# Idle products and new order edges at the start of a hybrid decoder step

## The chip, the cores and the metric

One Trainium2 chip, and on it one core. The metric is the device time of one execution in microseconds (us); a time is the median of several runs. The engines are PE (TensorE, matrix products), ACT (ScalarE), DVE (VectorE), POOL (GpSimd) and SP (SyncE, which only issues transfers). ACT and POOL issue transfers too; a queue that waits to issue one holds up the compute instructions behind it.

## What is computed

One layer of a hybrid decoder for 512 prompt tokens and 8 x 8 sample tokens (576 columns in all), all in float32:

```
h = x + 0.5 * SwiGLU_1(rms(x))                      # first FFN, 1024 -> 2816 -> 1024
u = rms(h) @ W_in -> z | xBC | dt | q | k | v | f | g_ssd | g_att
y_ssd = Mamba-2 SSD(z, xBC, dt)                     # causal conv of 4 on x/B/C, chunked scan, gate, group norm
y_att = FoX attention(q, k, v, f)                   # samples attend 2048 cached positions in pages
h = h + W_out(sigmoid(g_ssd) * (y_ssd @ W_ssd_proj) + sigmoid(g_att) * (y_att @ W_attn_proj))
y = h + 0.5 * SwiGLU_2(rms(h))                      # second FFN
```

The outputs are y for both groups, the new keys, values and log forget rows, and the new SSD and convolution states.

## The kernel before

The hidden state lies transposed in SBUF, features on the 128 partitions, the 576 tokens in the columns, in 8 tiles `hts[k]`. Every large product is made in three passes of one-pass float32 (`mm3`): each operand is split into a rounded half and the rest (`whi`, `wlo` for weights, `xh`, `xl` for activations), and the three products hi x hi, hi x lo and lo x hi are added (lines L208, L209, L210). Each pass takes 128 x 128 weights against 288 columns, half of the tokens. Weights come by SP's queue as `stage` tiles of 512 KB; ACT makes `whi` (L173), DVE or POOL `wlo` (L174).

The order of the stages: x is loaded in two column halves on the queues of SP and ACT, with the first gate weights between them. PE transposes it (L432 for prompt rows, L438 for sample rows), the copies go to `hts` (L434 on ACT, L436 and L439 on DVE), and `Norm.add` makes `xh` (L220, ACT) and `xl` (L221, DVE). ACT squares the rows of x (L446) for the norm; a short chain on DVE and four small products give the scale `nrm1.r`, by which the accumulators of the first FFN are multiplied as they leave PSUM. Then come setup loads of small weights (`bb` L488 and L489, `al` L493, and rows), the state_conv rows `sc` with 24 small transposes (L515) and their store, and the cached log forget rows: a gather `lg` (L524), 16 scans `pf` on DVE (L529), one product with the page matrix (L535), 16 subtractions on POOL (L540) and 32 stores `pastD` on ACT's queue (L546).

The FFN (`ffn`) goes over 22 tiles f of 128 hidden features: gate product, silu, up product, and the product of both split again into `hh` and `hl`; after 12 and after the last 10 tiles the down projection over 8 output tiles j. Accumulators come from `acc()`, which in the FFN alternates between two `acc` banks and two `pv` banks; two `tr` banks and two `mm` banks (`sm()`) serve transposes and small products. After each f and each j the FFN advances a generator `beside` by one step: here `turns(4)`, which loads tiles of the SSD state (`h0`, called h in the trace), transposes them (L376) and stores them.

Attention runs in 37 hand-ordered steps on PE; each handles a quarter of a sample's cached keys (`turn_keys`: transposes L924, copies `kT` on ACT L926; scores L935) and one query block of a prompt pair (`scores`: products L861, exps on ACT L867; turns L879; values L892), with products of the gates and of z filled in between. Behind attention the sample columns of its results are copied from `ys` on POOL (L1114). Then six convolution tiles of the first SSD group follow (`conv_tile`: POOL copy L1129, accumulators to `xr` on DVE L1133 to L1140, a transpose L1146 and its copy L1148 on ACT), and the attention projection with the split results `yh` (L217) and `yl` (L218).

The order of the instructions on each engine is made by a planner: it simulates the program with costs of its own and takes, among what is ready, what stands first in the code; `soon()` raises a priority. In attention PE's order is that of the code.

Of the kernel before, what the change touches and what calls it, by code (L numbers as in the profile page):

```python
# [16 lines left out]
I32 = mybir.dt.int32  # L17
# [76 lines left out]
def build(ctx, tc, A, O):  # L94
# [58 lines left out]

    def hs(half):
        return slice(half * HT, (half + 1) * HT)
# [56 lines left out]
    def hilo(hp, view, tagh, tagl, scale=None, n=NT, bufs=None):  # L212

        hi = tl(hp, [P, n], F32R, tag=tagh, bufs=bufs)
        lo = tl(hp, [P, n], F32R, tag=tagl, bufs=bufs)
        if scale is None:
            act(hi, view, AF.Copy)  # L217
            V.tensor_tensor(lo, view, hi.bitcast(F32), ALU.subtract)  # L218
        else:
            act(hi, view, AF.Copy, scale=scale)  # L220
            V.scalar_tensor_tensor(lo, view, scale, hi.bitcast(F32), ALU.mult, ALU.subtract)  # L221
        return hi, lo
# [45 lines left out]
    class Norm:  # L268


        def __init__(self, wcol, sqp=None, xsp=xp):
            self.wcol, self.xs, self.n, self.sqp, self.xsp = wcol, [], 0, sqp, xsp

        def add(self, h, squares=True):
            k = self.n
            self.xs.append(hilo(self.xsp, h, "xh", "xl", scale=P1[:, self.wcol + k:self.wcol + k + 1]))
# [36 lines left out]
    def ffn(nrm, cg, wu, wd, hts, done, beside):  # L313

        cu = Cols(wu, 0)
        with pool("hid", reuse_waits="tile") as hidp, pool("ffnt", bufs=2, reuse_waits="tile") as fp:
            for lo_f, hi_f in ((0, 12), (12, NF)):
                hid = []
                for f in range(lo_f, hi_f):
# [5 lines left out]
                    for half in range(2):  # L325
                        a = acc()
# [38 lines left out]
    def turns(wait):  # L365
# [42 lines left out]

    with pool("h1", reuse_waits="tile") as hp:
        hts = [tl(hp, [P, NT], tag=f"h{k}") for k in range(8)]  # L410
        nrm1 = Norm(0)
        with pool("xin", side="right", reuse_waits="tile") as xi:
# [16 lines left out]
            for k in range(8):  # L429
                t = tr()  # L430
                for c in range(4):
                    nc.tensor.transpose(t[:, c * P:(c + 1) * P], xin[c][:, k * P:(k + 1) * P], ident)  # L432
# [10 lines left out]
            for c in range(5):  # L443
                n = P if c < 4 else NS
                junk = tl(xi, [P, D], tag="junk")
                act(junk[:n], xin[c][:n], AF.Square, accum_out=x0[:n, c:c + 1])  # L446
# [4 lines left out]
        with pool("setup2", side="right", reuse_waits="tile") as su:  # L451
# [36 lines left out]
            q.dma_start(out=bb[:32], in_=A["dt_bias"].rearrange("o h -> h o"))  # L488
            q.dma_start(out=bb[32:48], in_=A["b_f"].rearrange("o h -> h o"))  # L489
# [3 lines left out]
            q.dma_start(out=al[:32], in_=A["a_log"].rearrange("o h -> h o"))  # L493
# [14 lines left out]
            sc = tl(su, [24, CONV], tag="sc")  # L508
            for j in range(3):
                q.dma_start(out=sc[j * B:(j + 1) * B], in_=A["state_conv"][0, :, j, :])  # L510
            scT = tl(su, [P, 24, 24], tag="scT")
            for j in range(0, 24, 12):
                t = tr()
                for i in range(12):
                    nc.tensor.transpose(t[:, i * 24:(i + 1) * 24], sc[:, (j + i) * P:(j + i + 1) * P], ident[:24, :24])  # L515
                V.tensor_copy(scT[:, j:j + 12, :], t[:, :288].rearrange("p (i c) -> p i c", c=24))
            q.dma_start(out=scD, in_=scT)


        with pool("lg", side="right", reuse_waits="tile") as lp:  # L520
            pcol = tl(lp, [P, 1], I32, tag="pcol")
            nc.scalar.dma_start(out=pcol, in_=A["page_table"].rearrange("b n -> (b n)").unsqueeze(1))
            lg = tl(lp, [P, P, 16], tag="lg")
            G.indirect_dma_start(out=lg.rearrange("p s h -> p (s h)"), out_offset=None,  # L524
                                 in_=A["cache_logf"].rearrange("o n s h -> (o n) (s h)"),
                                 in_offset=bass.IndirectOffsetOnAxis(ap=pcol[:, :1], axis=0))
            pf = tl(lp, [P, 16, P], tag="pf")
            for h in range(16):
                V.tensor_tensor_scan(pf[:, h, :], C("one"), lg[:, :, h], 0.0, ALU.mult, ALU.add)  # L529
            tot = tl(lp, [P, 16], tag="tot")  # L530
            V.tensor_copy(tot, pf[:, :, P - 1])
            t = sm()
            page = tl(lp, [P, P], tag="page")
            nc.scalar.dma_start(out=page, in_=A["consts"][:, COFF["page"][0]:COFF["page"][0] + P])
            mm(t[:, :16], lhsT=page, rhs=tot, start=True, stop=True)  # L535
            st = tl(lp, [P, 16], tag="st")
            V.tensor_copy(st, t[:, :16])

            for h in range(16):
                G.tensor_tensor(lg.rearrange("p s h -> p (s h)")[:, h * P:(h + 1) * P].rearrange("p (q r u) -> p r q u", q=4, u=4),  # L540
                                pf[:, h, :].rearrange("p (r q u) -> p r q u", q=4, u=4),
                                st[:, h:h + 1].unsqueeze(2).unsqueeze(3).to_broadcast([P, 8, 4, 4]), ALU.subtract)
            lv = lg.rearrange("p s h -> p (s h)").rearrange("p (h q e) -> p h q e", h=16, q=4)
            for b in range(B):
                for q in range(4):
                    nc.scalar.dma_start(out=pastD[b, :, q].rearrange("h g e -> g h e"), in_=lv[b * NPG:(b + 1) * NPG, :, q, :])  # L546
# [955 lines left out]
```

## Time and profile before

| | |
|---|---|
| median of 3 runs | 1887.17 us (1885.02 to 1891.32) |
| the profiled execution | 1890.57 us, span 1888.4 us |
| PE busy | 1834.7 us (97%) |
| DVE, ACT, POOL busy | 1062.6, 746.2, 606.5 us |
| mean transfer rate | 143 GB/s |

A span is the time between the first and the last instruction of the profile; the execution is a little longer. Rows of the profile name line, engine, operation, tile written and tiles read. A row of a timeline begins with start and duration; in brackets at its end stand the idle time ahead of it and what ended that. A row of a window stands for a stretch: its length, then busy time and instructions of PE, PEld (weight loads of PE), DVE, ACT and POOL, the granted clock of PE, the share of the transfer engines and GB/s.

### The profile page before, as it was taken

What the parts mean: (1) busy time and instruction counts of PE and PEld (TensorE: products, weight loads), DVE (VectorE), ACT (ScalarE), POOL (GpSimd) and SP (SyncE); (2) the same over time, 40 slices, a digit from 0 to 9 for tenths busy, and PEclk for the clock granted to TensorE, in tenths of its full rate; (3) what the DMA queues carried; (4) which work ended last, traced back from release to release, by engine and by line L of the source; (5) the groups of instructions that cost most, each with busy time, mean ns of one, the idle gap of its engine ahead of it and who ended that gap; (6) DMA issues with size and microseconds to landing.
All of it is one profiled execution on the core that took longest, in us unless ns stands there. A gap on an engine that the chain in (4) does not pass through costs nothing.

```text
span 1888.4 us, 38769 instructions
## 1 busy us (share of the span) xinstructions
PE 1834.7 (97%) x15335; PEld 1729.5 (92%) x15335; DVE 1062.6 (56%) x2309; ACT 746.2 (40%) x1555; POOL 606.5 (32%) x681
## 2 busy tenths in 40 slices
PE   7999999999999999999999999999999999999998
PEld 7999999999889787888899898888989999999998
DVE  4544234434425677777655968787695544444442
ACT  4233223334323545545335645454433333223322
POOL 0432003322322344443323735656553332002210
PEclk9999999999999999999999999999999999999999
DMA  5453443445525678775456545354463444444432
GB/s 154 107 147 124 134 124 112 124 146 142 140 79 167 184 223 228 233 217 156 117 144 189 151 113 149 98 152 143 134 210 90 118 130 133 144 132 125 117 119 67
DMA packets 297722, 269.71 MB, mean 143 GB/s; under 512 B 55068, under 2 KB 262092, under 8 KB 297388
## 3 DMA queue, kind: packets, MB, share of 16 engines
q1 hardware_dynamic: 229712, 184.16, 34.9%
q10 hardware_dynamic: 57828, 46.10, 7.9%
q0 software_dynamic: 10000, 36.97, 6.3%
q8 instruction: 121, 1.98, 0.5%
q14 instruction: 61, 0.50, 0.1%
HBM read 223.72 MB, written 38.73 MB: 139 GB/s over the span
## 4 chain that ended last, share of the span: by engine, by line
PE 83%; DVE 7%; DMA 3%; ACT 3%; issue 2%; POOL 1%; ACTq 1%; SPq 0%; DVEq 0%; POOLq 0%
PE acc L208 16%; PE acc L209 16%; PE acc L210 15%; PE pv L209 8%; PE pv L208 8%; PE pv L210 7%; PE tr L935 2%; PE tr L924 1%; PE mm L861 1%; DMA ab<-cumD 1%; PE pv L892 1%; DVE kf L1159 1%; PE mm L879 1%; PE pv L973 1%; PE tr L376 1%
## 5 line engine op out<-in xcount | busy, mean ns | idle before, releaser
L173 ACT ACTIVATE whi<-stage 128x512 fp32r<-128x512 f32 (+2 forms) x474 | 294.7, 622 | 713.0 <-PE acc L209 605.2
L208 PE MATMUL acc<-xh,whi 128*128 128x288 f32 x1792 | 542.3, 303 | 8.4 <-ACT tt L1148 3.6
L209 PE MATMUL acc<-xl,whi 128*128 128x288 f32 x1792 | 533.8, 298 | 0.0
L210 PE MATMUL acc<-xh,wlo 128*128 128x288 f32 x1792 | 533.0, 298 | 0.0
L174 DVE TENSOR_TENSOR wlo<-stage,whi 128x512 fp32r<-128x512 f32 (+1 forms) x373 | 260.7, 699 | 268.1 <-ACT whi L173 251.1
L208 PEld LDWEIGHTS acc<-xh,whi 128*128 128x128 f32 x1792 | 339.5, 189 | 15.7 <-ACT tt L1148 7.7
L209 PEld LDWEIGHTS acc<-xl,whi 128*128 128x128 f32 x1792 | 339.7, 190 | 2.9 <-issue 2.7
L210 PEld LDWEIGHTS acc<-xh,wlo 128*128 128x128 f32 x1792 | 338.9, 189 | 1.1 <-issue 0.5
L174 POOL TENSOR_TENSOR wlo<-stage,whi 128x512 fp32r<-128x512 f32 (+1 forms) x101 | 138.4, 1370 | 287.7 <-ACT whi L173 275.5
L341 POOL TENSOR_TENSOR u<-u,s 128x288 f32<-128x288 f32 x88 | 81.5, 927 | 437.2 <-DVE u L340 379.8
L208 PE MATMUL pv<-xh,whi 128*128 128x288 f32 (+1 forms) x720 | 214.2, 298 | 1.7 <-ACT xh L220 1.5
L209 PE MATMUL pv<-xl,whi 128*128 128x288 f32 (+1 forms) x720 | 213.1, 296 | 0.0
L210 PE MATMUL pv<-xh,wlo 128*128 128x288 f32 (+1 forms) x720 | 212.6, 295 | 0.0
L208 PEld LDWEIGHTS pv<-xh,whi 128*128 128x128 f32 (+1 forms) x720 | 135.3, 188 | 2.3 <-ACT xh L220 1.8
L209 PEld LDWEIGHTS pv<-xl,whi 128*128 128x128 f32 (+1 forms) x720 | 135.1, 188 | 1.3
L210 PEld LDWEIGHTS pv<-xh,wlo 128*128 128x128 f32 (+1 forms) x720 | 135.2, 188 | 0.2
L208 PE MATMUL pv<-hh,whi 128*128 128x288 f32 x352 | 105.7, 300 | 0.0
L343 POOL TENSOR_TENSOR hl<-u,hh 128x288 fp32r<-128x288 f32 x88 | 79.4, 904 | 80.4 <-ACT hh L342 80.4
L209 PE MATMUL acc<-hl,whi 128*128 128x288 f32 x352 | 104.1, 296 | 0.0
L208 PE MATMUL acc<-hh,whi 128*128 128x288 f32 x352 | 104.1, 296 | 0.0
L209 PE MATMUL pv<-hl,whi 128*128 128x288 f32 x352 | 104.1, 296 | 0.0
L210 PE MATMUL acc<-hh,wlo 128*128 128x288 f32 x352 | 104.1, 296 | 0.0
(364 smaller groups left out, 3618.0 us busy)
## 6 DMA issues: line engine op xcount, KB each, us to landing
stage<-in_w_in_dram SPq DMA_DIRECT2D x52, 512.0 KB
stage<-in_ffn_w_up_dram SPq DMA_DIRECT2D x44, 512.0 KB
stage<-in_ffn_w_gate_dram SPq DMA_DIRECT2D x43, 512.0 KB
stage<-in_ffn_w_down_dram SPq DMA_DIRECT2D x40, 512.0 KB
h<-in_state_ssm_dram SPq DMA_DIRECT2D x64, 256.0 KB
hTD<-hT ACTq DMA_DIRECT2D x32, 256.0 KB
pb<-pastD SPq DMA_DIRECT2D x32, 256.0 KB
ab<-cumD SPq DMA_DIRECT2D x32, 256.0 KB
```

The lines of the kernel that those rows point to most:

```text
L173: act(hi, view, AF.Copy)
L174: e.tensor_tensor(lo, view, hi.bitcast(F32), ALU.subtract)
L208: mm(out, lhsT=hi, rhs=a, start=first and i == 0, stop=False)
L209: mm(out, lhsT=hi, rhs=b, start=False, stop=False)
L210: mm(out, lhsT=lo, rhs=a, start=False, stop=last and i == n - 1)
L341: G.tensor_tensor(u, u, sil[half], ALU.mult)
L343: G.tensor_tensor(hl[:, hs(half)], u, hh[:, hs(half)].bitcast(F32), ALU.subtract)
L376: nc.tensor.transpose(ps[:, b * P:(b + 1) * P], h0[:, b, :], ident)
L861: mm(s[:, :n], lhsT=q, rhs=ks[2 * self.p + e][:, :n], start=hl == 0, stop=hl == 1)
L879: nc.tensor.transpose(t[:, j * P:(j + 1) * P], lt[:, j * P:(j + 1) * P], ident)
L892: mm(self.ob[o:o + 32, i * P:(i + 1) * P], lhsT=vtok[j][:, v0:v0 + 32], rhs=self.pts[e][:, j * P:(j + 1) * P], start=j == 0, stop=j == i)
L935: mm(s[kv * 32:(kv + 1) * 32, :], lhsT=self.q(kv), rhs=self.kT[kv // 2], start=True, stop=True)
```

## The change

- Six products of a constant tile (448 columns, plain float32) are put on PE ahead of the transposes of x.
- A helper `behind(later, first)` adds an edge of order between two instructions. With it the first three squares of x stand behind the 4th, 6th and 7th `xh`, the loads of `bb` and `al` behind the 8th; the other two squares are made on DVE.
- The gate products of f=1 use a `tr` and an `mm` bank.
- The work on `sc` and `lg` moves into a generator `aside`, which the FFN advances beside its tiles; after it come the state turns, with `h0` loaded two tiles ahead.
- In each first quarter of attention the two exps stand behind the key copies.
- The sample copies of `ys` and the splits `yh`, `yl` stand behind the third convolution tile; `ys` lies in another pool.

```diff
+    def behind(later, first):
+        tc.add_manual_dep(later.ins, first.ins.name, mybir.DependencyInfo(mybir.DependencyClass.NoSync, mybir.DependencyReason.DATA), reason="order")
...
-                        a = acc()
+                        a = (tr, sm)[half]()[:, :HT] if f in more else acc()
...
+            tiles = []
             for t in range(16):
                 for h in range(2):
-                    h0 = tl(sp_, [P, 4, P], tag="h0", bufs=4)
-                    nc.sync.dma_start(out=h0, in_=ap3(A["state_ssm"][0], *place(h, t)))
+                    for n in range(len(tiles), min(2 * t + h + 3, 32)):
+                        tiles.append(tl(sp_, [P, 4, P], tag="h0", bufs=4))
+                        nc.sync.dma_start(out=tiles[n], in_=ap3(A["state_ssm"][0], *place(n % 2, n // 2)))
+                    if t + h == 0:
+                        yield
+                    h0 = tiles[2 * t + h]
...
+    idle = tl(tp, [P, NT], tag="sq", bufs=1)
+    V.memset(idle, 1.0)
+    warm = [mm(pv()[:, :NT - P], lhsT=idle[:, NT - P:], rhs=idle[:, :NT - P], start=True, stop=True) for _ in range(6)]
...
-                    nc.tensor.transpose(t[:, c * P:(c + 1) * P], xin[c][:, k * P:(k + 1) * P], ident)
+                    x = nc.tensor.transpose(t[:, c * P:(c + 1) * P], xin[c][:, k * P:(k + 1) * P], ident)
+                    if k == 0:
+                        behind(x, warm[-1])
...
-                act(junk[:n], xin[c][:n], AF.Square, accum_out=x0[:n, c:c + 1])
+                if c < 3:
+                    behind(act(junk[:n], xin[c][:n], AF.Square, accum_out=x0[:n, c:c + 1]), nrm1.insts[2 * c + 3 - c // 2])
+                else:
+                    V.tensor_tensor_reduce(junk[:n], xin[c][:n], xin[c][:n], 1.0, 0.0, ALU.mult, ALU.add, x0[:n, c:c + 1])
...
-            q.dma_start(out=bb[:32], in_=A["dt_bias"].rearrange("o h -> h o"))
+            behind(q.dma_start(out=bb[:32], in_=A["dt_bias"].rearrange("o h -> h o")), nrm1.insts[7])
...
+        def aside():
+            with pool("rows", side="right", reuse_waits="tile") as su:
+                sc = tl(su, [24, CONV], tag="sc")
+                for j in range(3):
+                    nc.scalar.dma_start(out=sc[j * B:(j + 1) * B], in_=A["state_conv"][0, :, j, :])
+                yield
+                yield
...
+            with pool("lg", side="right", reuse_waits="tile") as lp:
...
+                for _ in range(2):
+                    yield
...
+            yield from turns(1)
...
-        ffn(nrm1, cg, A["ffn1_w_up"][0], A["ffn1_w_down"][0], hts, done1, turns(4))
+        ffn(nrm1, cg, A["ffn1_w_up"][0], A["ffn1_w_down"][0], hts, done1, aside(), (1,))
...
-        ys = tl(ap, [P, 2, 4, NS], tag="ys")
+        ys = tl(yp, [P, 2, 4, NS], tag="ys")
...
-                        act(self.kT[p], t, AF.Copy)
+                        copy = act(self.kT[p], t, AF.Copy)
+                    for x in exps:
+                        behind(x, copy)
...
-                    new.turn_keys(jq)
+                    new.turn_keys(jq, cur.exps if jq == 0 else ())
...
-        for p in range(2):
-            for g in range(4):
-                G.tensor_copy(yt[p * 4 + g][:, NP:], ys[:, p, g, :])
...
+        convs.append((first, tanh, last))
...
-            yhl = [hilo(yhp, y, "yh", "yl", bufs=8) for y in yt]
+            yhl = []
+            for n, y in enumerate(yt):
+                c = G.tensor_copy(y[:, NP:], ys[:, n // 4, n % 4, :])
...
+                h = act(hi, y, AF.Copy)
+                for x, first in zip((c, h, V.tensor_tensor(lo, y, hi.bitcast(F32), ALU.subtract)), convs[2]):
+                    behind(x, first)
+                yhl.append((hi, lo))
```

More of the change, by code (lines that the diff above doesn't have):

```diff
@@ L219, in hilo @@
         else:
-            act(hi, view, AF.Copy, scale=scale)
+            h = act(hi, view, AF.Copy, scale=scale)
             V.scalar_tensor_tensor(lo, view, scale, hi.bitcast(F32), ALU.mult, ALU.subtract)
+            if insts is not None:
+                insts.append(h)
         return hi, lo
@@ L310, in build, with ffn @@
     upbD = tl(dram, [4, 2, NS, P], tag="upbD")
-    def ffn(nrm, cg, wu, wd, hts, done, beside):
+    def ffn(nrm, cg, wu, wd, hts, done, beside, more=()):
         cu = Cols(wu, 0)
@@ L492, in build @@
             V.memset(al, 0.0)
-            q.dma_start(out=al[:32], in_=A["a_log"].rearrange("o h -> h o"))
+            behind(q.dma_start(out=al[:32], in_=A["a_log"].rearrange("o h -> h o")), nrm1.insts[7])
             act(al, al, AF.Exp)
@@ L506, in build @@
             V.tensor_tensor(pidx, pf32.unsqueeze(2).to_broadcast([P, B, 4]), rq.unsqueeze(1).to_broadcast([P, B, 4]), ALU.add)
[L508 to L546, printed above, removed]
@@ L853, in scores @@
                 n = (i + 1) * P
-                self.lts = []
+                self.lts, self.exps = [], []
                 for e in range(2):
```

53 lines of the change are left out of this document (44 added, 9 removed).

## The prediction

> **What bounds the kernel now.** I read the page first. TensorE (PE) is busy for nearly the whole span, and the chain that ended last is 83% PE, so time can come only from PE's waits and from products that PE runs slowly.
>
> ```profile
> span 1888.4 us, 38769 instructions
> PE 1834.7 (97%) x15335; PEld 1729.5 (92%) x15335; DVE 1062.6 (56%) x2309; ACT 746.2 (40%) x1555; POOL 606.5 (32%) x681
> ```
>
> The span less PE's busy time is 53.7 us. The view of waits on PE says for whom (line, who released it, us in total, times, longest):
>
> ```profile
> PE tr L935 <- ACT kT L926: 5.2, 6, 1.1
> ...
> PE acc L208 <- ACT tt L1148: 3.8, 8, 1.8
> ...
> PE tr L257 <- POOL ssq L1246: 3.2, 1, 3.2
> ...
> PE tr L376 <- DMA h<-in_state_ssm_dram: 2.8, 1, 2.8
> ...
> PE tr L515 <- DMA sc<-in_state_conv_dram: 1.8, 1, 1.8
> ...
> PE mm L535 <- DVE tot L531: 1.3, 1, 1.3
> ...
> PE acc L1146 <- POOL xr L1129: 1.3, 1, 1.3
> ```
>
> All but L257 lie in places that the diff touches: the row work before the first FFN (L515, L535, L376), attention (L935), and the first convolution tiles after it (L1148, L1146). The fourth place is the start. A wait has a second price, which the stretches by window show (us, PE busy, ..., granted clock):
>
> ```profile
> 14.78:33.11 18.33, 18.33 (x115) 17.39 (x116) 13.07 (x34) 13.72 (x25) 0.00 (x0) 1.00 0.32 95
> 33.11:35.34 2.23, 1.66 (x13) 1.29 (x11) 1.80 (x4) 1.41 (x4) 0.00 (x0) 1.00 0.20 17
> 103.85:110.40 6.55, 3.71 (x18) 3.74 (x18) 2.44 (x4) 1.86 (x5) 4.27 (x5) 0.74 0.76 222
> 921.90:930.00 8.10, 5.39 (x27) 5.20 (x28) 6.85 (x12) 4.50 (x9) 1.56 (x3) 0.79 0.01 2
> ```
>
> Around the waits for L376 and for the convolution tiles the granted clock averages 0.74 and 0.79: a half-rate spell. The timeline of PE shows what half rate is in the start, where the clock column says 1.00 all the same:
>
> ```profile
> 17.04 0.44 PE L208 MATMUL pv<-xh,whi 128*128 128x288 f32 x1
> 17.28 0.44 PE L209 MATMUL acc<-xl,whi 128*128 128x288 f32 x1
> 24.20 0.29 PE L208 MATMUL pv<-xh,whi 128*128 128x288 f32 x1
> 24.33 0.30 PE L209 MATMUL pv<-xl,whi 128*128 128x288 f32 x1
> 52.42 0.44 PE L209 MATMUL pv<-xl,whi 128*128 128x288 f32 x1
> 55.30 0.44 PE L209 MATMUL pv<-xl,whi 128*128 128x288 f32 x1
> ```
>
> From start to start a product of 288 columns takes 0.24 us at half rate, 0.13 us else. From 52.42 to 55.30 thirteen products are slow: 13 x 0.11 = 1.4 us for one spell. In the start products are slow from 14.78 to about 21.5.
>
> **Part 1, the start: 4.5 us.** The chain of waits, then the timelines of PE, DVE and ACT, and a plain f32 product in the chain:
>
> ```profile
> 3.97 9.59 DMA stage<-in_ffn_w_gate_dram
> 13.57 0.33 ACTq L488
> 13.96 0.78 ACT xh L220
> 14.78 0.61 PE pv L208
> ...
> 7.70 0.47 PE L438 MATMUL mm<-ident,xin 64*128 64x64 f32 x2 [2.21 <-DMA xin<-in_x_sample_dram]
> 10.18 0.69 DVE L436 COPY h<-tr 128x512 f32<-128x512 f32 x1 [1.03 <-PE tr L432]
> 10.96 1.06 ACT L446 ACTIVATE junk<-xin 128x1024 f32<-128x1024 f32 x1
> 1071.07 1.05 PE mm L1331 x2
> ```
>
> The first copy of x (h, L436) is ready at 10.87, but its half xh runs at 13.96: ACT does a square first (1.06 us), then its queue stands before the issue of L488 until the gate weight of its own queue has landed (3.97 + 9.59 = 13.56). The change puts the squares behind the fourth, sixth and seventh half, and the three small loads behind the eighth, so xh can run when h is there, and the first product about 0.8 us later: at 11.7 instead of 14.78 if nothing holds x back.
>
> The six idle products can. They are plain f32; L1331 shows one of 512 columns (two instructions) in 1.05 us, so one of 448 takes 0.92 us at full rate and 1.84 at most at half: 6 of them 5.5 to 11.0 us. With a memset ahead they begin near 1.2 and end between 6.7 and 12.2; with half rate for one spell of 3.1 us it is 1.2 + 3.1 + (6 - 1.7) x 0.92 = 8.3, with the 6.7 us of the old start 1.2 + 6.7 + (6 - 3.6) x 0.92 = 10.1. PE waited for x until 7.7 (L438), so I take x at PE around 9.5 and the first real product at 12.2, 2.6 us earlier. Bounds: 0.3 to 3.1 us.
>
> What follows: 115 instructions took 18.33 us up to 33.11. At full rate 96 products x 0.132 and 19 transposes of about 0.11 are 14.8 us, 3.5 less. If the clock stays up, some of this is lost to x's production (eight ACT halves and DVE halves, whose engines are 13.7 and 13.1 us busy in that stretch), so I take 1.3, between 0 and 3.5. The two squares on DVE cost its queue 2 to 4 us (an estimate: once to twice ACT's 1.06 us each); PE's 96 products hide them, as these end after the norm is ready, and without that cover they would be paid in full.
>
> The first gate tile of f=1 in tr and sm banks gives PE work while the norm r is spread: 2.23 us between 33.11 and 35.34 hold about 1.3 us of work, so 0.6 to 0.9 is left to gain; I take 0.6, as one of the two banks turns free only after the setup transposes. Sum 2.6 + 1.3 + 0.6 = 4.5; ends 0 and 7.
>
> **A rule on the clock.** The rows above say only that half rate follows pauses of 1.8 us and more. The Trainium skill, "TensorE: Matmul & The Clock Gate", Part 1, says that the clock rises after one busy window of about 3.4 us and falls after an idle one; its Part 4 says that transposes do not count as busy. By it the transposes of x, which alone fill the time from the last idle product to the first real one, would let the clock fall if that takes over 3.4 us; I take it as shorter, and the other outcome is rival A.
>
> **Part 2, the row work moved beside the FFN (aside): 4.5 us.**
>
> ```profile
> 43.01 6.64 DMA sc<-in_state_conv_dram
> ...
> 98.67 4.70 DMA pastD<-lg
> ...
> 106.69 0.87 PE tr L376 x4
> ...
> L546 ACTq DMA_DIRECT2D pastD<-lg x32: 309/462/1151, 81.2 to 98.7; - x32
> 71.16 0.40 PE L535 MATMUL mm<-tot,page 128*128 128x16 f32 x2 [1.33 <-DVE tot L531]
> ```
>
> The state_conv load now has two weight tiles (96 products x 0.132 = 12.7 us each) before its transposes are due, against a landing of 6.6 us: the wait of 1.8 and its spell of 1.4 go. The page product L535 likewise stands two tiles behind its scans: 1.3 goes. 1.8 + 1.4 + 1.3 = 4.5, between 3 and 4.5. Moved with it: three loads and a store on ACT's queue (0.3 us each at issue), the 32 pastD stores on the same queue (17.5 us from 81.2 to 98.7), the gather on POOL, 16 scans on DVE; all run beside full PE stretches now and I cost them at nothing. Behind the stores on ACT stand the FFN's hh halves; PE does not need those before the down projection. If that cover were gone, the 17.5 us would show.
>
> The state turns (L376) wait 2.8 and pay a spell of 1.4, 4.2 in all. Their loads go to memory that the stores still read, so they begin only when the last store has landed: 35.5 us from the page product at 71.16 to 106.69. The change prefetches two tiles more on SP's queue, but behind the same stores; only the transposes are due one tile later, two tiles (25.4 us) after the page product. 25.4 is less than 35.5 and PE stood 32.4 us away before, so the order already went by the planner's idea of the stores, not by the place in the code. I leave the wait where it is: gain 0, between -3 and 4.2. Late next after it are the SP weight loads queued behind these tiles, which are a tile pair ahead.
>
> **Part 3, attention: exps behind the key copies, 4.5 us.**
>
> ```profile
> 651.33 1.41 ACT L L867 x4
> ...
> 652.65 1.05 ACT L926 ACTIVATE kT<-tr 128x512 f32<-128x512 f32 x2
> 653.27 1.10 PE L935 MATMUL tr<-kT,qz 128*32 128x512 f32 x6 [0.96 <-ACT kT L926]
> 658.67 1.04 PE L879 MATMUL mm<-ident,L 128*128 128x128 f32 x8
> ```
>
> At each first quarter the two exps (1.41 us) stand ahead of the copies kT, and PE waits 0.96. Swapped, the copies come 1.41 earlier, more than the longest wait (1.1), so all six waits (5.2) go. Behind the exps stand the sums and scales on DVE, then PE's turn L879 at 658.67: the exps would end near 653.7, 5 us before. I keep 4.5: DVE and DMA may take back the rest. Ends 3 and 5.2.
>
> **Part 4, the first convolution tiles: 3.5 us.**
>
> ```profile
> 921.46 2.00 POOL L1129 COPY xr<-scT 128x24 f32<-128x24 f32 x3
> 919.84 4.13 ACT L217 ACTIVATE yh<-qy 128x576 fp32r<-128x576 f32 x7 [1.28 <-POOL qy L1114]
> 920.56 4.84 DVE L218 TENSOR_TENSOR yl<-qy,yh 128x576 fp32r<-128x576 f32 x7 [0.85 <-ACT yh L217]
> 938.00:945.00 7.00, 6.90 (x52) 6.59 (x51) 5.68 (x10) 2.99 (x6) 2.25 (x4) 1.00 0.02 4
> ```
>
> The copies of ys, then yh and yl, stand ahead of the first convolution tiles on POOL, ACT and DVE, while PE waits 1.3 (L1146, for L1129) and 1.8 (L1148) and pays a spell of 1.4 (0.79 granted from 921.9): 4.5. Behind the third tile they no longer can. But all eight must be there for the attention projection, three tiles later, and in a tile DVE has 7.00 - 5.68 = 1.3 us free, 3 x 1.3 = 4 us for 8 x 0.69 = 5.5: PE may wait 1 to 1.5 us there. I take 3.5, between 0 and 4.5. The move of ys to the other pool costs nothing by itself.
>
> **Sum.** 4.5 + 4.5 + 4.5 + 3.5 = 17 us off a span of 1888.4, whose execution took 1890.57. The median of the runs is 1887.17, 3.4 lower; I take the gain off the median: 1870.
>
> **Rivals.** A: the idle products do not pay; they end late and the clock still falls. The start then gives 1.5 (0.3 earlier, 0.6 at r, 0.6 of rate): 1873. For it: the transposes of L515 after 1.8 idle did not keep the clock up at 52.42. Chance 0.12.
> B: the turns' wait goes as well, if the prefetch makes the planner put them late enough: 17 + 4.2, 1866. Against it: the same stores. 0.17.
> C: yl before the projection costs PE more than the conv tiles gain: part 4 gives -1, 1874.5. For it: 1.3 us free a tile. 0.12.
> D: the change does not do what it says. The order of every queue comes from a planner's own times, and what it moves in untouched stages can give back most of it: the scan stage has one wait of 3.2 (L257), and three more like it, each with a spell, 3 x 4.6 = 14, leave 3: 1884. 0.12.
> E, slower: the planner puts the turns nearer to the page product than the stores allow. PE then waits 35.5 us less the planned distance; against the 17 gained elsewhere it decides from a wait of 2.8 + 17 = 20 us, a distance of 15. At 10 us of distance it is 25.5, 22.7 more than now: 1887 - 17 + 22.7 = 1893. Against it: two tiles in the code, 25.4. With all unknown mishaps 0.09.
>
> **How the numbers follow.** The forecast holds 0.38, with its own range of 1866 to 1875. Over 0.3% (5.7 us, about what these runs can tell) faster are the forecast, A, B and C: 0.79; D is the same, 0.12; E is slower, 0.09. The range goes from all upper ends (7 + 4.5 + 4.2 + 5.2 + 4.5 = 25.4, 1862) up into D, 1883, and leaves out under 2 in 10.
>
> **What would show it.** First real product near 12 with 0.13 us steps (A: 0.24); L488 no longer ahead of xh; no wait at L515, L535; at L376 still about 2.8 (B: none, E: over 10); no wait of L935 for kT; L1129 near the first tile, and a new wait for yl at the projection (C: over 2 us). Wrong if waits over 2 us appear between 970 and 1400.

## The result and the profile after

The changed kernel takes 1871.74 us (median of 1869.64 to 1872.73) where the kernel before takes 1887.72 (1885.02 to 1891.32): a ratio of 0.9913, 95% interval 0.9894 to 0.9932. The forecast was 1870. The profiled execution took 1872.17 us, 1870.2 of it span.

The sum came out, but not by its terms. The start, which was to give 4.5 us, cost some; attention gave more than twice what was expected; and of the 16.2 us by which attention differs in the first two profiles, some 4.6 turned out to be no effect of the change at all.

The page's head, as before (span, then busy time by engine):

```profile
span 1870.2 us, 38796 instructions
PE 1829.8 (98%) x15347; PEld 1727.7 (92%) x15347; DVE 1063.7 (57%) x2314; ACT 740.4 (40%) x1551; POOL 606.0 (32%) x681
```

The span less PE's busy time went from 53.7 to 40.4 us. The waits on PE, by line and releaser (us in total, times, longest):

```profile
PE acc L212 <- DVE xr L1160: 4.0, 3, 1.8
...
PE tr L1404 <- ACT oo L1394: 3.8, 2, 2.3
...
PE tr L387 <- DMA h<-in_state_ssm_dram: 3.5, 1, 3.5
...
PE tr L249 <- DVE rsy L242: 2.0, 1, 2.0
...
PE acc L1173 <- DVE xr L1167: 1.6, 2, 1.0
```

No row is left for the key copies (5.2 before), for sc (1.8) and for tot (1.3). The turns (L387, before L376) still wait for their loads. New is the wait for the norm's root rsy (2.0). Three waits grew: for xr behind DVE at L1160 (L1133 before) from 2.9 to 4.0 and at L1167 (L1140 before) from 0.6 to 1.6, and for oo at L1404 (L1365 before) from 1.4, at most 1.0 at a time, to 3.8, at most 2.3.

The start, on PE and ACT (start, us, engine, line, operands; idle time before and its releaser in brackets):

```profile
1.53 4.85 PE L423 MATMUL pv<-sq 128*128 128x448 f32 x6 [1.53 <-DVE al L512]
...
8.16 1.77 PE L423 MATMUL pv<-sq 128*128 128x448 f32 x4
...
10.13 1.02 PE L423 MATMUL pv<-sq 128*128 128x448 f32 x2
10.98 1.04 PE L447 MATMUL tr<-ident,xin 128*128 128x128 f32 x8
17.78 0.61 PE L212 MATMUL pv<-xh,whi 128*128 128x288 f32 x1
35.67 1.13 PE L249 MATMUL tr<-ident,rsy 128*128 128x128 f32 x8 [1.98 <-DVE rsy L242]
14.47 0.63 ACT L177 ACTIVATE whi<-stage 128x512 fp32r<-128x512 f32 x1 [3.73 <-DMA stage<-in_ffn_w_gate_dram]
16.46 1.44 ACT L224 ACTIVATE xh<-h,P 128x576 fp32r<-128x576 f32 x2 [0.88 <-DVE h L453]
```

The idle products end at 11.15, x's transposes begin behind them (8.81 in the profile before), and the first real product comes at 17.78, 3.0 later than before, not 2.6 earlier. ACT shows why: the second split of the gate weight now stands ahead of x's copies, and ACT's queue stood 3.73 us for that weight. The first row below, a window of the first products (us, PE busy, ..., granted clock), shows that the idle products did not keep the clock up either:

```profile
17.78:20.25 2.47, 2.47 (x12) 2.45 (x12) 2.03 (x6) 2.47 (x6) 0.00 (x0) 0.53 0.02 6
...
919.00:940.00 21.00, 17.47 (x129) 16.78 (x128) 19.06 (x32) 12.55 (x22) 5.18 (x7) 1.00 0.27 56
```

The second row is the stage of the late yh and yl: full clock here, but DVE is busy 19.06 of 21 us, and its yl stand ahead of the convolution's own xr:

```profile
922.93 3.44 DVE L1222 TENSOR_TENSOR yl<-qy,yh 128x576 fp32r<-128x576 f32 x5
926.79 0.40 PE L212 MATMUL acc<-xh,whi 128*128 128x288 f32 x1 [1.70 <-DVE xr L1160]
934.43 0.35 PE L1173 MATMUL acc<-ident,xr 128*91 128x128 f32 x1 [1.02 <-DVE xr L1167]
```

### The profile page after: what moved, and what is told of

It reads as the page before. It is cut to its first block, busy times and chain, and to the rows that moved or that the text cites. A ratio compares the mean times of both kernels' runs of the same rounds, so it can differ in the third digit from the quotient of the medians.

```text
span 1870.2 us, 38796 instructions
## 1 busy us (share of the span) xinstructions
PE 1829.8 (98%) x15347; PEld 1727.7 (92%) x15347; DVE 1063.7 (57%) x2314; ACT 740.4 (40%) x1551; POOL 606.0 (32%) x681
## 4 chain that ended last, share of the span: by engine, by line
PE 64%; DVE 5%; DMA 2%; ACT 2%; issue 1%; POOL 0%; SPq 0%; ACTq 0%; DVEq 0%; POOLq 0%
PE acc L212 13%; PE acc L214 13%; PE acc L213 13%; PE pv L213 4%; PE pv L214 4%; PE pv L212 4%; PE tr L966 2%; DMA ab<-cumD 2%; PE tr L953 1%; PE mm L889 1%; PE pv L920 1%; PE mm L907 1%; PE pv L1357 1%; PE tr L993 1%; PE pv L1004 1%; PE mm L1370 1%
## 5 line engine op out<-in xcount | busy, mean ns | idle before, releaser
L178 DVE TENSOR_TENSOR wlo<-stage,whi 128x512 fp32r<-128x512 f32 (+1 forms) x373 | 262.9, 705 | 270.4 <-ACT whi L177 250.0
L178 POOL TENSOR_TENSOR wlo<-stage,whi 128x512 fp32r<-128x512 f32 (+1 forms) x101 | 138.2, 1369 | 283.0 <-ACT whi L177 253.1
```

The lines of the kernel that those rows point to most:

```text
L178: e.tensor_tensor(lo, view, hi.bitcast(F32), ALU.subtract)
```

## The experiments

Runs 1 to 4 share a chip, called A here, 5 to 8 chip B, and 9 to 12 chip C; each chip was used in one session only, so "chip" below means a chip and its session. The chips of the first two profiles are not on record. On A the kernel before took 1889.46 us (7 runs), on B 1884.62 (7), on C 1889.31 (9). Lengths are from each kernel's own profile: r is when the spread of the norm begins (first product of ident and rsy), "down" the first product of hh, attention goes from the first product of Ks and qs to the last transpose of oz, and conv from there to the first product of yh (to the last transpose's end for both).

| kernel | chip | us, median | ratio to before, 95% | first real product | r | down | attention | conv |
|---|---|---|---|---|---|---|---|---|
| before, first profile | - | 1887.72 | | 14.8 | 33.1 | 190.8 | 301.8 | 41.1 |
| after, first profile | - | 1871.74 | 0.9913 (0.9894 to 0.9932) | 17.8 | 35.7 | 189.0 | 285.6 | 38.9 |
| 1 exps alone | A | 1881.4 | 0.9958 (0.9942 to 0.9975) | 14.8 | 31.9 | 188.3 | 296.0 | 41.0 |
| 2 all but exps | A | 1880.48 | 0.9945 (0.9927 to 0.9964) | 15.7 | 33.8 | 185.8 | 299.7 | 38.1 |
| 3 old start | A | 1871.59 | 0.9906 (0.9889 to 0.9922) | 14.8 | 32.0 | 183.1 | 290.0 | 38.9 |
| 4 no idle products | A | 1874.97 | 0.9933 (0.9914 to 0.9952) | 11.7 | 31.5 | 183.6 | 291.7 | 40.4 |
| 5 split behind xh | B | 1869.58 | 0.9918 (0.9899 to 0.9936) | 14.4 | 32.3 | 182.3 | 287.3 | 40.4 |
| 6 no idle, root first | B | 1867.56 | 0.9908 (0.9892 to 0.9925) | 12.3 | 29.9 | 179.2 | 286.3 | 38.9 |
| 7 exps and conv alone | B | 1878.06 | 0.9955 (0.9937 to 0.9972) | 14.0 | 31.8 | 191.2 | 289.8 | 38.1 |
| 8 no idle, wlo behind kf | B | 1869.05 | 0.9918 (0.9895 to 0.9942) | 11.9 | 32.0 | 185.5 | 285.8 | 40.1 |
| 9 before again | C | 1890.39 (one run) | | 15.5 | 33.2 | 190.2 | 302.9 | 41.0 |
| 10 after again | C | 1876.35 | 0.9918 (0.9902 to 0.9933) | 16.2 | 34.7 | 187.2 | 290.7 | 40.4 |
| 11 four steps | C | 1868.96 | 0.9882 (0.9863 to 0.99) | 12.5 | 30.6 | 178.8 | 292.5 | 39.9 |
| 12 idle, order mended | C | 1872.71 | 0.9914 (0.9899 to 0.9928) | 14.8 | 32.6 | 183.3 | 292.7 | 38.9 |

Each row's lengths come from one execution. The kernel before and the runs 1 and 7 have the same start and the same first FFN, and so has run 9; their r lies between 31.8 and 33.2 and their first down product between 188.3 and 191.3. A difference of 1 us at r or of 3 us at the first down product between two single rows can be chance.

**1 and 2: where does attention's gain come from?** Run 1 is the kernel before with the edges of the exps alone, run 2 the changed kernel without them.

```
# run 1, into before
                    for x in exps:
                        behind(x, copy)
# run 2, in after
-                    new.turn_keys(jq, cur.exps if jq == 0 else ())
+                    new.turn_keys(jq, ())
```

> The kernel before with one thing of the change: in each first quarter of attention the two exps stand behind the key copies. Theory X (the edges alone bring what attention gained, 301.8 to 285.7 us from the first key scores to the last sample turn, also what the view of waits did not show): 15 us off, about 1873 us. Rival Y (the edges bring only the six shown waits, 5.2 us; the rest comes from ys in the other pool and the later splits): about 1882.5 us.

> The changed kernel without the edges behind the key copies. Theory X: attention loses about 15 us again, 1887 us. Rival Y: about 5 us, 1877 us, and attention stays near 291 us.

Attention fell by 5.8 us with the edges alone and by 2.1 with all the rest; the first profiles differ by 16.2. Neither theory makes 16.2 out of that. The answer lies in the lengths of the steps of attention, from one group of kk transposes to the next. The edges take 1.1 to 1.4 us off six of the first-quarter steps, 7.7 us in all. But the last five fourth-quarter steps are 8.5 to 9.7 us long in before and in runs 1 to 4, and 8.05 in the profile after. Summed over seven such steps, it is 60.0 us in before, 62.0 in run 1, 60.5 in run 2, and 55.5 in after. So run 1 gave 2 of its 7.7 back there, and the profile after has 4.6 there that neither run has.

**3 and 4: does the start pay?** Run 3 has the old start (no idle products; squares, loads and the f=1 banks as before), run 4 leaves out the idle products alone.

```
# run 4, in after
-    warm = [mm(pv()[:, :NT - P], lhsT=idle[:, NT - P:], ...) for _ in range(6)]
...
-                    if k == 0:
-                        behind(x, warm[-1])
```

> The changed kernel with the old start: no idle products, all squares on ACT without edges, the loads of bb and al free, no extra banks. Theory S (the new start costs 2 to 3 us: first real product 3.0 later, norm r 2.6 later and a half-rate spell behind it): first product near 14.8, 1869 us. Rival T (the start pays, and the time was lost by the moved row work): first product near 14.8 too, but 1874 us or more.

> The changed kernel without the six idle products alone. Theory S (they hold the transposes of x 2.2 us back, and the planner then puts ACT's second gate split ahead of the copies of x): first product 15 or earlier, 1869 to 1870 us, with slow products up to about 21. Rival R (the full rate they bring is worth more than the delay): 1873 us or more.

Run 2, on the same chip, has the start of the changed kernel: r at 33.8 and the first down product at 185.8. Run 3 has them at 32.0 and 183.1, run 4 at 31.5 and 183.6. Run 4 has its first real product at 11.65, where the forecast put it "if nothing holds x back" (11.7), and yet gains nothing on the old start: r comes at 31.5 in the one and 32.0 in the other. PE waits 2.98 for it in run 4 and not at all in run 3: the norm's root ends at 31.4 in run 4 and at 30.1 in run 3, although run 4's products begin 3.1 earlier. So in the new start the end of this stage is the norm r, which ACT and DVE make, and not the first product. At r the old start is 1.8 us better than the new one on chip A, and the five kernels with the old start (31.8 to 33.2) all lie before the three with the whole new one (33.8 to 35.7): Part 1 as a whole cost time. In whole times this is not clear of the noise: run 3 is at 0.9906 of before, the changed kernel at 0.9913 and 0.9918, and the intervals overlap. Run 4's time of 1874.97 lies on theory R's side, but not for its reason, since in the changed kernel the first products ran at 0.53 with the idle products ahead; run 4's executions spread from 1871.83 to 1880.77, and its profile is the fastest of them.

**5 and 6: what delays the start?** Run 5 puts the second gate split behind x's second half; run 6 has no idle products and puts the seventh and eighth weight splits on DVE behind the norm's root.

```
# run 5, in split()
+            if turn[0] == 2:
+                behind(h, nrm1.insts[1])
# run 6, in split()
+            if turn[0] in (7, 8):
+                behind(low, norm_end[0])
```

> The changed kernel with one more edge: the second split of the first gate weight (whi) on ACT is put behind the second half of x (xh). Theory Q: the idle products cost what they cost because the planner, seeing x later, set that split ahead of x's copies, and ACT's queue then stood until 14.47 for the gate weight (3.73 us of wait). Then the first real product comes at about 14 instead of 17.78, the first down product 2 to 4 us earlier (185 to 187 instead of 189.0), and the time is 1868 to 1870. Rival I: the delay is that of the idle products themselves (x's transposes begin at 10.98 instead of 8.8 behind them); ACT then only waits elsewhere, the first real product stays after 16.5, the first down product within 1 us of 189, and the time at 1871 to 1873.

> The changed kernel without its idle products (as in the run of that name), and with the seventh and eighth weight splits on DVE put behind the last instruction of the norm's root. In that run two splits stood between the root's instructions (28.53 and 29.21, the first waiting 0.90 for ACT) and PE waited 2.98 for the spread, with nine slow products behind it (33.63 to 35.55). Theory R (the wait for r and its spell are what is left in the start): the spread begins about 1.5 us earlier, at 30, PE's wait there is 1.5 or less, the spell gets shorter or goes, the first down product comes at 181 to 182 instead of 183.55, and the time is 1869 to 1870 in its best run. Rival P: another wait takes its place (the splits are then late for the next gate tile); the first down product stays within 0.5 us of 183.5.

Run 5, ACT and PE, and on PE and DVE two rows out of attention for run 8 below:

```profile
12.04 1.43 ACT L226 ACTIVATE xh<-h,P 128x576 fp32r<-128x576 f32 x2
13.37 0.62 ACT L177 ACTIVATE whi<-stage 128x512 fp32r<-128x512 f32 x1
14.38 0.38 PE L214 MATMUL pv<-xh,whi 128*128 128x288 f32 x1
14.38:17.00 2.62, 2.62 (x23) 2.38 (x22) 2.62 (x5) 2.16 (x4) 0.00 (x0) 1.00 0.83 266
...
801.36 2.53 DVE L1059 SCALAR_TENSOR_TENSOR kf<-sq,kf 128x576 f32<-128x576 f32 x1
805.96 0.66 PE L955 MATMUL tr<-ident,kk 128*128 128x128 f32 x4 [1.17 <-DVE PTs L997]
```

Theory Q holds: one edge moves x's halves from 16.46 to 12.04, the first product from 17.78 to 14.38 and the first down product from 189.0 to 182.3. (These are compared with the first profile after, whose chip is not known; on C, run 12 against run 10, the same edge and the one of run 6 give 3.9.) Run 6 holds theory R:

```profile
29.93 1.13 PE L254 MATMUL tr<-ident,rsy 128*128 128x128 f32 x8 [0.78 <-DVE rsy L245]
```

On the same chip run 8, whose start has neither edge, waits 2.98 for r and spreads it at 31.98, with 13 slow products behind; run 6 waits 0.78, has no spell there, and is 2.1 us earlier at r. At the first down product it is 6.3 us earlier (179.2 against 185.5), but not all of this is the edge's: run 8 also waits longer for the state turns (2.48 against 1.69) and has 14 slow products behind that wait, where run 6 has none.

**7: is the convolution part the partner of the exps?** The kernel before with the exps' edges, the ys in the other pool and the late yh, yl; start and row work as before.

> The kernel before, with two parts of the change: the exps behind the key copies, and the move of ys with the late yh and yl. Neither the start nor the row work is changed. Alone the exps took 5.8 us off attention (301.8 to 296.0), all other parts together 2.1, both 10 to 16. Theory C: the partner is the convolution part (ys and yh, yl no longer press on attention's end); attention, from the first key scores to the last turn of a sample, takes 290 to 292 us, the stage after it up to the projection 38 to 39 us instead of 41, and the time is 1873 to 1875. Rival F: the partner is the phase in which each fourth step of attention meets POOL's work, which any change before it shifts; attention stays at 294 to 298, and the time is 1877 to 1881.

Attention came to 289.8, in theory C's interval, but for neither reason: its fourth-quarter steps sum to 55.7, as in all four kernels of chip B (55.5 to 55.7), run 6 and run 8 with quite other starts among them. That pointed at the chip rather than at any edit, which the runs 9 and 10 put to the test. The time, 1878.06, is in theory F's interval (1877 to 1881) and not in C's.

**8: is it POOL's split that makes these steps long?** On top of run 4, POOL's split waits for the product on DVE that ends a z tile.

```
+            if e is G and kfdone:
+                tc.add_manual_dep(low.ins, kfdone.pop().ins.name, ... Sync ...)
```

> The changed kernel without its idle products, and in attention POOL's split of a weight (wlo, 1.28 us) waits for the product on DVE that ends a z tile (kf from sq and kf). In the fourth steps this product took 0.76 us where POOL's split did not run beside it and 1.98 to 2.46 us where it did, and those steps were 9.2 to 9.6 us long instead of 8.5. Theory D: the collision is what makes these steps long. Then the product takes under 1.1 us in all of them, the steps with a sample's fourth quarter are 8.5 us or less throughout (three were 9.3 to 9.5), attention takes 288 to 289 us instead of 291.7, and the time is 1868 to 1870, with less spread between runs than the 9 us that the kernel without idle products showed. Rival B: the late step is due to POOL's bias and gathers, which stay where they are; the steps stay at 9.3 to 9.5 and the time at 1872 to 1875.

As a test the run is inconclusive: its fourth-quarter steps are 8.05 to 8.1, but so are those of its neighbours without this edge, and run 6 has no stretched product either. The rows of all runs say more. On B the product is stretched twice, to 2.53 us in run 5 and to 2.28 in run 7; the steps that hold it are 8.06, but the first-quarter steps behind them are 9.26 and 9.02, where the others behind a fourth quarter are 7.65 to 7.77. In run 5 PE stands 1.17 at 805.96 for PTs, the copy that DVE makes late behind the product. Run 8 has no product over 1.04 and no such step over 7.75. On A, on C and in the first profile before, the third to the sixth fourth-quarter steps hold a product of 1.8 us or more 18 times, and all 18 are 8.79 to 9.65 long; of the other 18, twelve are 8.49 to 8.55, one is 8.84, and five, all at the fourth place, are 9.53 to 9.65 for a reason that is not known. So the stretch makes a step long, its own or the next: theory D's mechanism is borne out by this count, if not by its edge, which was not run on A or C.

**9 and 10: the same two kernels on one chip.**

> The kernel before, unchanged, for a profile on the same chip as the three runs beside it. The fourth-quarter steps of attention took 8.5 to 9.7 us in the profile of before and in four runs of one chip, whatever their edits, and 8.05 to 8.1 us in the profile after and in four runs of another chip, whatever their edits. Theory K (it is the chip): before and the changed kernel show the same lengths here, so of the 16.2 us by which attention differs in the two first profiles some 4.6 are not the change's, and before's attention is 297 to 298 us where the changed kernel's is 285 to 287. Rival L (it is the kernel, and the edits of the second chip all had it): before shows 8.5 to 9.7 here and the changed kernel 8.05.

> The changed kernel, unchanged, beside the two variants of it, for times on one chip. Theory K: fourth-quarter steps as in before on this chip; the start as in its first profile, first real product after 17, first down product 188 to 190; the time 1870 to 1872, and 12 to 16 us under before. Rival L: attention shorter than before's by 16 on this chip too.

Theory K holds in the point that parts it from L: on chip C the seven fourth-quarter steps sum to 59.9 in before and 59.1 after. Its other numbers missed: attention was 302.9 and 290.7 (not 297 to 298 and 285 to 287), and the changed kernel took 1876.35 (not 1870 to 1872). The same program shows both forms. Profile after, then after again on C, at the same place of the step:

```profile
700.90 0.29 DVE L893 CUSTOM_DVE_ANT_0 L<-bias,mm 128x128 f32<-128x128 f32 x1 [0.37 <-PE mm L889]
702.80 0.45 DVE L1028 COPY ys<-tr 64x64 f32<-64x64 f32 x2
703.09 1.03 PE L953 MATMUL tr<-ident,kk 128*128 128x128 f32 x8
```

```profile
701.06 0.29 DVE L893 CUSTOM_DVE_ANT_0 L<-bias,mm 128x128 f32<-128x128 f32 x1 [0.97 <-PE tr L993]
702.92 0.45 DVE L1028 COPY ys<-tr 64x64 f32<-64x64 f32 x2
703.51 0.63 PE L953 MATMUL tr<-ident,kk 128*128 128x128 f32 x4 [0.26 <-DVE ys L1028]
708.33 2.53 DVE L1057 SCALAR_TENSOR_TENSOR kf<-sq,kf 128x576 f32<-128x576 f32 x1
708.95 1.29 POOL L178 TENSOR_TENSOR wlo<-stage,whi 128x512 fp32r<-128x512 f32 x1
```

On C, DVE gets the scores 0.6 us later, so ys is copied beside the kk transposes instead of ahead of them, PE waits 0.26 for the bank, and everything on DVE behind it runs about 0.45 later, where POOL's split can meet it. Why the scores come later on A and C than on B stays open.

So the fair comparison is this one. Before again, then after again (first real product, r, first down product, first scores, last transpose of oz, first product of the projection):

```profile
15.51 0.61 PE L208 MATMUL pv<-xh,whi 128*128 128x288 f32 x1 [2.21 <-ACT xh L220]
33.21 1.05 PE L243 MATMUL tr<-ident,rsy 128*128 128x128 f32 x8
190.24 0.38 PE L208 MATMUL pv<-hh,whi 128*128 128x288 f32 x1
614.72 1.17 PE L861 MATMUL mm<-Ks,qs 128*128 128x512 f32 x4
917.36 0.27 PE L990 MATMUL tr<-ident,oz 128*128 128x128 f32 x1
958.65 0.29 PE L208 MATMUL acc<-yh,whi 128*128 128x288 f32 x1
```

```profile
16.18 0.45 PE L212 MATMUL pv<-xh,whi 128*128 128x288 f32 x1
34.69 1.13 PE L249 MATMUL tr<-ident,rsy 128*128 128x128 f32 x8 [2.09 <-DVE rsy L242]
187.20 0.38 PE L212 MATMUL pv<-hh,whi 128*128 128x288 f32 x1
613.93 1.18 PE L889 MATMUL mm<-Ks,qs 128*128 128x512 f32 x4
904.37 0.27 PE L1021 MATMUL tr<-ident,oz 128*128 128x128 f32 x1
945.08 0.30 PE L212 MATMUL acc<-yh,whi 128*128 128x288 f32 x1
```

Start to r: -1.5. From r to the first down product: 157.0 to 152.5, +4.5. From there to the first scores: -2.25. Attention: +12.2. Conv: +0.6. From the projection to the end, the rest of the spans' difference (1888.2 to 1876.6): -1.9. The sum is 11.6. Both profiles are single executions; the one of the changed kernel, at 1878.57, is the slowest of its five, so a term can be off by some us. In runs 11 and 12 on this chip attention is 292.5 and 292.7, 10.4 and 10.2 under before.

**11 and 12: what is left.** Run 11 is run 6 with two steps more: the turns one tile later, and three of the eight yl on POOL, the eight spread over two tiles. Run 12 has the idle products, with the edges of runs 5 and 6.

```
# run 11
-            yield from turns(1)
+            yield from turns(2)
...
+                low = (G if n < 3 else V).tensor_tensor(lo, y, hi.bitcast(F32), ALU.subtract)
+                for x, k in ((c, 0), (h, 1), (low, 0 if n < 3 else 2)):
+                    behind(x, convs[2 + (n > 4)][k])
```

> The changed kernel without idle products, with the two splits behind the norm's root (as in the run before last of that name), the state turns one tile later, and three of the eight yl on POOL, spread with the others over two convolution tiles. Each step is read in its own stage. Start: first real product near 12, r spread near 30, first down product 178 to 180 after the turns' part. Turns: the stores of the page work end 17 to 18 us after the page product, and the turns waited 1.7 to 3.5 us; 12.7 us later they wait for nothing, and the spell of 14 products behind the wait goes (theory T: 2 to 4 us in the first FFN); rival U: the planner puts them no later, the wait stays at 2. Convolution: the waits for xr behind the yl on DVE were 1.7, 1.0 and 0.8 us; theory V: with three yl on POOL they come to 1.5 together, the stage up to the projection takes 37 us instead of 38.9; rival W: POOL's yl stretches DVE's work or comes late, and the stage stays at 38.5 or more. Time by T and V: 1863 to 1865; by U and W 1867.

> The changed kernel with its idle products, the second gate split behind x's second half, and the two splits behind the norm's root; no other edit. Theory M (with the order mended the idle products neither help nor hurt, since the start then ends with the norm r, which comes from ACT and DVE): r is spread at 30 to 31.5, the wait for it is under 1 us, the first down product comes within 1.5 us of the variant without idle products less its gain at the turns, and the time is 1865 to 1868. Rival N (they pay): r at 29 or before, first down product 178 or before. Rival O (they cost by themselves, as x's transposes stand behind them): first real product 14.4 or later, r after 31.5, first down product after 182.

Run 11: the first state turn stands without a wait, and the spell of 14 products that runs 10 and 12 have behind it is gone (T). From r to the first down product it takes 148.2 us, against 150.7 in run 12 and 152.5 in run 10. The convolution step failed (W), and the time, 1868.96, is above both forecasts (1863 to 1865, and 1867):

```profile
125.78 0.60 PE L392 MATMUL tr<-ident,h 128*128 128x128 f32 x4
920.41 3.26 POOL L1223 TENSOR_TENSOR yl<-qy,yh 128x576 fp32r<-128x576 f32 x2 [4.23 <-ACT yh L1222]
925.53 0.40 PE L215 MATMUL acc<-xh,whi 128*128 128x288 f32 x1 [1.42 <-DVE xr L1161]
```

POOL needs 1.6 us for one yl, DVE's two still stand ahead of each xr, and PE waits 1.42 for the first of the two and 1.06 for the second. Run 12 goes by O: first real product 14.8, r at 32.6, first down product 183.3. With the order mended the idle products still cost 2 us at r (30.6 in run 11). On one chip, run 11's time is 7.4 us under the changed kernel's (1868.96 against 1876.35), with no overlap of their runs; run 12's is 3.6 under, and there the runs overlap.

## Why the prediction came out, step by step

**Part 1, the start, failed.** Forecast +4.5; measured at r -1.5 on C (run 10 against 9) and -1.8 on A (run 2 against 3). The failing step is "I take x at PE around 9.5 and the first real product at 12.2". Three of the six products ran at half rate and three at full, as was worked out (4.85, 1.77 and 1.02 us), but the planner put x's sample transposes in between, PE waited 1.31 us there, and the last product ended at 11.15 instead of 8.3 to 10.1. Worse, with x due later the planner put the second gate split ahead of x's copies on ACT, an order that the diff does not name; runs 5 and 12 show its price. The step behind it was wrong too: an earlier first product buys nothing while r ends the stage. The 2 to 4 us of squares on DVE were costed at nothing: "PE's 96 products hide them, as these end after the norm is ready". The norm was ready after them: PE waits 2.0 for rsy, and where that wait was 2.0 to 3.0 us a spell of 9 to 14 slow products followed in runs 2, 4, 5, 8 and the profile after (in run 10 none did). The squares took 1.23 us each on DVE, within the estimate; what came on top was the order: in run 4 two weight splits on DVE stood between the instructions of the root, and run 6, with the squares still on DVE and the two splits behind the root, has the wait at 0.78 where run 8 has 2.98. The f=1 banks alone were not run.

Rival A ("they end late and the clock still falls") is what happened, with a lower price than real, since r was not in it. Between the last idle product's end and the first real product lay 6.6 us in the profile after, 5.6 in run 2, 5.5 in run 10, 4.7 in run 12 and 3.75 in run 5. The granted clock behind fell to about 0.5 in the first four (from 16.2 on in run 12), and stayed 1.00 in run 5. The Trainium skill, "TensorE: Matmul & The Clock Gate", Parts 1 and 4, has the clock fall after an idle window of about 3.4 us, with transposes not counted as busy; the four gaps of 4.7 us and more agree, x's transposes being nearly all that PE did in them. The spells behind waits of 1.7 to 3.0 us came after less idle time than that: in run 9 a wait of 1.71 for the page product (L535) is followed by 15 slow products.

**Part 2, the row work, was right in its mechanism, and its number in part by luck.** Forecast 4.5; from r to the first down product the one-chip profiles differ by 4.5. The waits for sc and tot are gone, and the turns' wait stayed, so rivals B and E are out. On C the two waits (1.78 and 1.71) and the spells behind them (13 and 15 products at 0.11 us) were some 6.6 us. The turns, whose gain was taken as 0, cost some 3 of these: their wait went from 1.9 to 3.4, with a spell of 14 products behind it that before again does not have. What is left to the 4.5, some 0.9, is open; the f=1 banks (forecast 0.6) may be in it. No run has the row work alone. Run 11 shows that the wait goes one tile later; the order in the code does move it, which the forecast doubted.

**Part 3, attention, was under-sized.** The six waits were taken for the price, 5.2 us. Attention gave 12.2 on C. The term that was mis-sized is the single step: the copies came 1.41 earlier and the step got 1.4 shorter, not 0.7 to 1.1. Before again and after again, kk transposes that begin and end one first-quarter step:

```profile
648.82 1.03 PE L924 MATMUL tr<-ident,kk 128*128 128x128 f32 x8
652.62 1.10 PE L935 MATMUL tr<-kT,qz 128*32 128x512 f32 x6 [0.97 <-ACT kT L926]
653.56 0.60 PE L935 MATMUL tr<-kT,qz 128*32 128x512 f32 x2
657.16 1.03 PE L924 MATMUL tr<-ident,kk 128*128 128x128 f32 x8
```

```profile
645.16 1.03 PE L953 MATMUL tr<-ident,kk 128*128 128x128 f32 x8
646.93 1.06 ACT L955 ACTIVATE kT<-tr 128x512 f32<-128x512 f32 x2
647.89 0.72 ACT L895 ACTIVATE L<-L,mn 128x512 f32<-128x512 f32 x1
647.93 1.17 PE L966 MATMUL tr<-kT,qz 128*32 128x512 f32 x8
652.10 1.04 PE L953 MATMUL tr<-ident,kk 128*128 128x128 f32 x8
```

8.34 against 6.94. The first score waits 0.97 for the first copy, and the last two scores come 0.37 late for the second copy, in a place where the view of waits shows none. Seven such steps give 8.4 on C. That is with one stretched product in run 10, whose next first-quarter step is 8.99. Of the rest, 2.7 lie before and in the first step of attention, where every kernel with the row work aside is shorter, after 2.25 lost just ahead of the first scores; by its size this is time that moved, not time saved, though no run shows what moved. In the first two profiles another 4.6 were the fourth-quarter steps'.

**Part 4, the convolution, was over-sized.** Forecast 3.5; 2.1 to 2.9 in the kernels without a half-rate spell in this stage, 0.6 to 0.9 in those with one (run 11 left aside). No wait for yl stands at the projection: it came earlier, in the tiles, as 1.7 and 1.0 for xr behind DVE's yl. A wait of 1.13 for xr stood in these tiles before as well (L1133 at 918.18), which the forecast did not count. The arithmetic of DVE's free time (1.3 us a tile for 5.5 us of yl) was right; the place was not.

**The sum** was 17 and is 11.6 in the one-chip profiles (13.0 in the times there, 1889.31 to 1876.35) and 16.0 in the first times. Part 1's error of 6 and some 1.9 given back behind the projection (rival D's mechanism at a seventh of its price; PE's wait for oo there was 1.8 us in before again and 2.9 in after again, and in the first profile after one of them was 2.3, at 1224.88, which the prediction had named as a sign of being wrong) were covered by attention. The value was right by errors that cancel.

## What to carry to other kernels

Before a faster start is priced, ask what ends the stage: here it was the norm on ACT and DVE, and a first product 3 us earlier was worth nothing until two splits were moved behind the norm's root. An added delay also changes what a planner puts ahead in an in-order queue, so look for queues whose next entry waits on a load. Compare two profiles only from one chip and session, or check that untouched places have the same lengths in both, before a difference is given to an edit.

## What was not expected of the hardware

- Three chips, one session each: seven fourth-quarter steps of attention sum to 55.5 to 55.7 us on B and 59.1 to 62.0 on A and C, whatever the edits, and the kernel before takes 1884.62 us on B against 1889.46 and 1889.31.
- DVE's kf product took 0.75 us by itself and 1.8 to 2.53 in 20 cases beside POOL's split of 1.3 us (L1057 at 708.33 with L178 at 708.95, above). In all 20 it ends 0.62 to 0.63 us behind the split's end, however far it had begun before it (up to 0.62 us), as if nearly all of its work were done after the split. The Trainium skill, "Trainium Architecture — The Big Picture", section "What this means for kernel authors", has the two engines share a port pair under an exclusive lock; the rows agree. The price shows in a step of attention, on A and C in the one that holds the product, on B in the next one (9.26 and 9.02 us instead of 7.7).
- Without idle products the start's first products ran at half rate in some runs and not in others: in run 6 they step by 0.24 us from 12.66 to 14.11, and the clock column says 1.00 all the same, as in the old start; in run 4 they step by 0.13 to 0.14 from 12.03 on.
